# Two mixers of a one-core transformer kernel: low weight parts on another engine, branches interleaved, the triangular inverse spread between projections

## The chip, the cores and the metric

The kernel runs on one core of a Trainium2 chip. Such a core has TensorE (matmuls, written PE in the profile, its weight loads PEld), VectorE (DVE), ScalarE (ACT), GpSimd (POOL) and SyncE (SP), which here issues the transfers between memory and the core's own SBUF. Matmuls write to PSUM, which has eight banks. The metric is the time of one execution in microseconds (us).

## The reference

Two networks follow each other on 512 tokens of width 1024, all in float32. The first has two layers of: gated feed-forward, mixer, gated feed-forward; the second has attention, pooling, cross-attention and feed-forwards. Only the two mixers are touched. A mixer projects the normed tokens once and splits the columns:

```
proj = rmsnorm(x, mix_norm) @ w_in                     # 1024 -> 3600 columns
q, k, v, z, beta, alpha, hy = split(proj)
qkv  = silu(dwconv5(q, k, v));  q, k = l2norm(q), l2norm(k)
o_dn = delta_rule(q, k, v, beta, alpha), both directions  # chunked, needs the inverse of a
                                                       # unit triangular matrix per chunk and head
o_dn = rmsnorm(o_dn) * silu(z)
v, x1, x2 = dwconv3(hy) + bias                         # three streams
o_hy = rmsnorm(x2 * (h2 conv (x1 * (h1 conv v + d1 v)) + d2 ...))   # long filters by Fourier matrices
x = x + concat(o_dn, o_hy) @ w_out
```

## The kernel before, in words

**Precision by parts.** TensorE multiplies float32 matrices here in rounded form, so each operand is split in a high part (rounded by ScalarE) and a low part (the difference). A product is three matmuls (`acc3`, L330 to L336): high by high, high weight by low activation, low weight by high activation. For weights this is `load_w`: a transfer into `wr` (L302), then `split`: `wh` by ScalarE (L288) and `wl = wr - wh` (L289) by the engine that the caller names with `lo`. VectorE is the default; the mixer's projections name GpSimd.

**Projections of the mixer.** 28 weight tiles of 1024 x 128 (`proj`, 8 x 3 matmuls of 512 columns each): 12 heads (4 each of q, k, v), 12 streams of the hyena branch, 4 gates z. The result stands in a PSUM bank; VectorE multiplies it by the token norm `r`. A head then gets a convolution of five taps (`conv`: one on ScalarE, four on VectorE at L567), a tanh on ScalarE and a last product on VectorE; a stream three taps (two on VectorE); a gate a tanh and a product. Streams and gates are spilled to memory and read back later. A projection takes one of three PSUM banks (`pj`, `pj`, `pk`).

**Delta rule.** From k come per chunk of 128 tokens and per direction the matrices A (`decay`: matmuls, ScalarE's abs and exp, GpSimd's two mask products L864 and L868, VectorE's L866). `inverse` writes the 32 x 32 diagonal blocks of A to memory and reads them back with one block per partition (`L`), runs 31 steps of forward substitution on VectorE (two instructions each, L991 and L993), sends the result back through memory (L997 to L1004) and joins blocks by small matmuls (L1016 to L1042). `scan` then walks over four chunks in both directions (L1059 to L1095).

**Hyena.** `spectrum` makes the filters (L664, L665: high and low part of the filter's weights; L666 the decay, GpSimd's sums, L674 the transform). `hyena_run` convolves (L697, L715, L733) with products on VectorE (L719 to L742). The output projection is `half_proj`: first the half of its inputs from the delta rule, then the half from the hyena.

**What sets the order.** The program is recorded in the order of the code, and a scheduler then orders each engine's instructions by a model of their times, in the bounds of data, buffers and banks; each engine runs its own row in order. So code written later can stand earlier in a row. Transfers are all in SyncE's row.

Of the kernel before, what the change touches and what calls it, by code (L numbers as in the profile page):

```python
# [9 lines left out]
F32 = mybir.dt.float32  # L10
F32R = mybir.dt.float32r
ACTF = mybir.ActivationFunctionType
ALU = mybir.AluOpType
# [217 lines left out]
class Net:  # L231
# [395 lines left out]
    def filter_out(self, i, o, cs, th, tl):  # L627
        nc = self.nc
        wo = self.tmp("ssq", bufs=1)
        wov = self.a[f"flt{i}"][:, 196:].rearrange("p (d o c) -> p d o c", d=2, o=2)[:, :, o, cs]  # L630
        for e in range(2):
            nc.sync.dma_start(wo[64 * e:64 * e + 64].rearrange("p (d c) -> p d c", d=2), wov)
        wh = self.tmp(th, dt=F32R)
        wl = self.tmp(tl, dt=F32R)
        nc.scalar.copy(wh, wo)
        nc.vector.tensor_sub(wl[0:64], wo[0:64], wh[0:64].bitcast(F32))
        return wh, wl

    def spectrum(self, pool, i, hs, first, spec):
        nc, a = self.nc, self.a  # L640
# [12 lines left out]
        for o in range(2):  # L653
            for half in range(2):
                cs = slice(256 * half, 256 * half + 256)
                wh, wl = first if o == half == 0 else self.filter_out(i, o, cs, "t", "u")
                for lt in range(4):
                    dec, f = decs[n1 % 4], fb[n1 % 2]
# [3 lines left out]
                    for e, hs in ((0, fwd[lt]), (1, bwd[lt])):  # L662
                        es = slice(256 * e, 256 * e + 256)
                        nc.tensor.matmul(p[:, es], hs, wh[:, es], start=True, stop=False)  # L664
                        nc.tensor.matmul(p[:, es], hs[0:64], wl[0:64, es], start=False, stop=True)  # L665
                    nc.vector.tensor_mul(f, p.rearrange("p (d c) -> p d c", d=2), dec)  # L666
# [138 lines left out]
    def mixer(self, pool, i, spec, nrm):  # L805
        nc, a = self.nc, self.a
        win = a[f"win{i}"]
# [61 lines left out]

        for n, base, tag in (("k", 4, "k2"), ("v", 8, "v2"), ("q", 0, "q2")):  # L870
            qkv[n] = pool.tile([128, 4, S], F32, name=f"{n}2{i}", tag=tag)
            k2, v2 = qkv["k"], qkv.get("v")
            for h in range(4):
                p = self.proj(win[base + h], act, lo=nc.gpsimd)
                t, c, s = self.tmp("t"), self.tmp("u"), self.tmp("s")
                nc.vector.tensor_mul(t, p, r)
                self.conv(c, t, [self.col(f"dn_conv{i}", 12 * k + base + h) for k in range(5)])
                nc.scalar.activation(s, c, ACTF.Tanh, scale=0.5)
                nc.vector.scalar_tensor_tensor(qkv[n][:, h, :], s, 1.0, c, ALU.add, ALU.mult)
                if (n, h) == ("k", 1):  # L880
                    ba = self.mixer_small(i, act)
                elif (n, h) == ("v", 0):
                    pn["k"] = norms("k")
                elif (n, h) == ("v", 1):
                    be, g, G, ekd, egl, eg = self.mixer_gates(pool, i, ba, rt)
                elif n == "q":
                    if h == 0:
                        rates()
                    decay(h)
        Mc = self.inverse(pool, i, A, N)  # L890
        pn["q"] = norms("q")
        q2 = qkv["q"]
        nc.vector.tensor_scalar(epq, pn["q"], 4e-6, 1.28e-4, ALU.add, ALU.mult)
        for c in range(4):
# [4 lines left out]
            for d in range(2):  # L899
                nc.vector.tensor_tensor(at[:, d, c], hd(qk), at[:, d, c], ALU.mult)  # L900


# [15 lines left out]
        first = self.filter_out(i, 0, slice(0, 256), "a", "b")  # L918
        for t in range(3):
            for h in range(4):  # L920
                p = self.proj(win[16 + 4 * t + h], act, lo=nc.gpsimd)
                tt, c = self.tmp("t"), self.tmp("u")
                nc.vector.tensor_mul(tt, p, r)
                self.conv(c, tt, [self.col(f"hy_conv{i}", 12 * k + 4 * t + h) for k in range(3)],
                          self.col(f"hy_conv_bias{i}", 4 * t + h))
                nc.sync.dma_start(spill[(3, 0, 1)[t], h], c)
        for h in range(4):
            p = self.proj(win[12 + h], act, lo=nc.gpsimd)
            t, s = self.tmp("t"), self.tmp("s")
            nc.vector.tensor_mul(t, p, r)  # L930
            nc.scalar.activation(s, t, ACTF.Tanh, scale=0.5)
            nc.vector.scalar_tensor_tensor(t, s, 1.0, t, ALU.add, ALU.mult)
            nc.sync.dma_start(spill[2, h], t)

        o = pool.tile([128, 4, 4, 128], F32, name=f"o{i}", tag="v2")
# [32 lines left out]
    def inverse(self, pool, i, A, N):  # L968
# [17 lines left out]
        nc.gpsimd.memset(wf, 0.0)  # L986
        nc.gpsimd.memset(wf[:, 0:1024:33], 1.0)
        for k in range(31):
            n, m = 31 - k, k + 1
            t = T[:, 0:n * m].rearrange("p (a b) -> p a b", a=n)  # L990
            nc.vector.tensor_tensor(t, L[:, k + 1:, k:k + 1].to_broadcast([128, n, m]),  # L991
                                    W[:, k:k + 1, 0:m].to_broadcast([128, n, m]), ALU.mult)
            nc.vector.tensor_tensor(W[:, k + 1:, 0:m], W[:, k + 1:, 0:m], t, ALU.subtract)  # L993
        WT = pool.tile([128, 32, 32], F32, name=f"WT{i}", tag="L")
        nc.vector.tensor_copy(WT, W.rearrange("p r c -> p c r"))
# [592 lines left out]
```

## Time and profile before

| | us |
|---|---|
| median of three runs | 3795.7 (3792.1 to 3802.3) |
| the profiled execution's own time | 3800.8 |
| its span | 3799.0 |
| TensorE, VectorE, ScalarE, GpSimd busy | 3684.7, 2122.5, 1341.5, 976.1 |
| first mixer: first and last matmul of its projections | 392.6 to 640.6 |
| second mixer: the same | 1583.8 to 1827.9 |

A window of the profile gives for each engine its busy time and instructions, and the granted clock of TensorE as a share of 2.4 GHz. A matmul's row shows a duration longer than the distance to the next, since matmuls overlap; rates are therefore taken from counts in a stretch or from starts that follow each other. "a <- b" in a wait is the instruction that waited and what ended its wait.

### The profile page before, as it was taken

What the parts mean: (1) busy time and instruction counts of PE and PEld (TensorE: products, weight loads), DVE (VectorE), ACT (ScalarE), POOL (GpSimd) and SP (SyncE); (2) the same over time, 40 slices, a digit from 0 to 9 for tenths busy, and PEclk for the clock granted to TensorE, in tenths of its full rate; (3) what the DMA queues carried; (4) which work ended last, traced back from release to release, by engine and by line L of the source; (5) the groups of instructions that cost most, each with busy time, mean ns of one, the idle gap of its engine ahead of it and who ended that gap; (6) DMA issues with size and microseconds to landing.
All of it is one profiled execution on the core that took longest, in us unless ns stands there. A gap on an engine that the chain in (4) does not pass through costs nothing.

```text
span 3799.0 us, 45466 instructions
## 1 busy us (share of the span) xinstructions
PE 3684.7 (97%) x17516; PEld 2969.6 (78%) x17516; DVE 2122.5 (56%) x3190; ACT 1341.5 (35%) x2009; POOL 976.1 (26%) x705
## 2 busy tenths in 40 slices
PE   8999989999999999998999999999999999899998
PEld 6878767888888878767887888877788888688886
DVE  4344695774334443486675344667666464866464
ACT  3223432133223323352223233346444343444342
POOL 2111353431021201253442112477101011510011
PEclk9999998999999999998999999999999999999999
DMA  3232333522323233423343232410423334323322
GB/s 119 89 101 88 126 106 108 168 78 94 94 92 94 91 95 91 143 81 114 116 161 98 88 110 90 135 40 32 142 90 106 95 94 121 118 68 95 94 94 83
DMA packets 178816, 383.95 MB, mean 101 GB/s; under 512 B 40550, under 2 KB 83302, under 8 KB 177576
## 3 DMA queue, kind: packets, MB, share of 16 engines
q1 hardware_dynamic: 178600, 381.06, 32.1%
q8 instruction: 137, 2.24, 0.3%
q14 instruction: 79, 0.65, 0.1%
HBM read 347.97 MB, written 33.03 MB: 100 GB/s over the span
## 4 chain that ended last, share of the span: by engine, by line
PE 83%; DVE 11%; issue 2%; DMA 2%; ACT 2%; POOL 1%; SPq 0%; DVEq 0%; ACTq 0%; POOLq 0%
PE pj L331 10%; PE pj L330 10%; PE pj L336 8%; PE pk L331 5%; PE pk L330 5%; PE pa L330 4%; PE ps L330 4%; PE pa L331 4%; PE ps L331 4%; PE ps L336 4%; PE pa L336 4%; PE pk L336 4%; DVE u L567 3%; PE pj L333 2%; PE pk L333 1%
## 5 line engine op out<-in xcount | busy, mean ns | idle before, releaser
L288 ACT CAST wh<-wr 128x1024 fp32r<-128x1024 f32 x612 | 590.2, 964 | 1146.3 <-PE pj L331 462.6
L289 DVE TENSOR_TENSOR wl<-wr,wh 128x1024 fp32r<-128x1024 f32 (+1 forms) x554 | 626.6, 1131 | 483.0 <-PE pj L336 125.7
L514 POOL TENSOR_TENSOR t<-s,u 128x512 f32<-128x512 f32 x88 | 175.9, 1999 | 1072.9 <-DVE u L513 967.6
L331 PE MATMUL pj<-xl_ffn_norm,wh 128*128 128x512 f32 x856 | 339.8, 397 | 3.9 <-DVE xl_ffn_norm L292 3.9
L330 PE MATMUL pj<-xh_ffn_norm,wh 128*128 128x512 f32 x856 | 339.3, 396 | 0.0
L375 POOL TENSOR_TENSOR ssq<-ssq,c 128x512 f32<-128x512 f32 x76 | 113.3, 1491 | 489.2 <-ACT c L372 460.0
L336 PE MATMUL pj<-xh_ffn_norm,wl 128*128 128x512 f32 x856 | 217.7, 396 | 0.0
L289 POOL TENSOR_TENSOR wl<-wr,wh 128x1024 fp32r<-128x1024 f32 x58 | 146.9, 2534 | 225.6 <-ACT wh L288 195.0
L548 POOL TENSOR_TENSOR t<-t,s 128x512 f32<-128x512 f32 x44 | 58.0, 1318 | 569.2 <-DVE s L567 499.9
L331 PEld LDWEIGHTS pj<-xl_ffn_norm,wh 128*128 128x128 f32 x856 | 161.1, 188 | 44.3 <-DVE xl_ffn_norm L292 6.0
L330 PEld LDWEIGHTS pj<-xh_ffn_norm,wh 128*128 128x128 f32 x856 | 161.3, 188 | 40.6 <-issue 1.6
L336 PEld LDWEIGHTS pj<-xh_ffn_norm,wl 128*128 128x128 f32 x856 | 160.9, 188 | 39.1 <-issue 0.8
L288 ACT CAST hh_ffn_norm<-t 128x512 fp32r<-128x512 f32 x132 | 81.5, 618 | 307.2 <-POOL t L514 303.0
L330 PE MATMUL pk<-xh_ffn_norm,wh 128*128 128x512 f32 x472 | 187.1, 396 | 0.6 <-ACT wh L288 0.6
L567 DVE SCALAR_TENSOR_TENSOR u<-t,vec,u 128x511 f32<-128x511 f32 (+1 forms) x144 | 169.9, 1188 | 31.1 <-ACT u L561 22.0
L331 PE MATMUL pk<-xl_ffn_norm,wh 128*128 128x512 f32 x472 | 187.0, 396 | 0.0
L289 DVE TENSOR_TENSOR hl_ffn_norm<-t,hh_ffn_norm 128x512 fp32r<-128x512 f32 x132 | 92.2, 699 | 164.7 <-ACT hh_ffn_norm L288 164.7
L331 PE MATMUL pj<-hl_ffn_norm,wh 128*128 128x512 f32 x396 | 157.0, 397 | 0.0
L330 PE MATMUL pj<-hh_ffn_norm,wh 128*128 128x512 f32 x396 | 156.9, 396 | 0.0
L330 PE MATMUL ps<-xh_ffn_norm,wh 128*128 128x512 f32 x384 | 152.6, 397 | 0.0
L330 PE MATMUL pa<-xh_ffn_norm,wh 128*128 128x512 f32 x384 | 152.4, 397 | 0.0
L331 PE MATMUL ps<-xl_ffn_norm,wh 128*128 128x512 f32 x384 | 152.2, 396 | 0.0
(792 smaller groups left out, 8689.7 us busy)
## 6 DMA issues: line engine op xcount, KB each, us to landing
wr<-in_cu SPq DMA_DIRECT2D x88, 512.0 KB, 3.5
wr<-in_win SPq DMA_DIRECT2D x56, 512.0 KB, 3.6
wr<-in_ffn2g SPq DMA_DIRECT2D x44, 512.0 KB, 3.5
wr<-in_ffn2u SPq DMA_DIRECT2D x44, 512.0 KB, 3.5
wr<-in_ffn1g SPq DMA_DIRECT2D x43, 512.0 KB, 3.4
wr<-in_ffn1u SPq DMA_DIRECT2D x43, 512.0 KB, 3.5
wr<-in_ffn1d SPq DMA_DIRECT2D x32, 512.0 KB, 3.5
wr<-in_ffn2d SPq DMA_DIRECT2D x32, 512.0 KB, 3.5
```

The lines of the kernel that those rows point to most:

```text
L288: nc.scalar.copy(h, src)
L289: lo.tensor_sub(l, src, h.bitcast(F32))
L330: mm(out, sh, mh, start=first and i == 0, stop=False)
L331: mm(out, sh, ml, start=False, stop=False)
L333: mm(out, sl, mh, start=False, stop=last and i == n - 1)
L336: mm(out, sl, mh, start=False, stop=last and i == n - 1)
L375: (nc.gpsimd if k < n - 1 else nc.vector).tensor_add(ssq, ssq, sq)
L514: nc.gpsimd.tensor_mul(t, s, u)
L548: nc.gpsimd.tensor_mul(t, t, cs[1])
L567: nc.vector.scalar_tensor_tensor(out[:, a:b], t[:, a + d:b + d], taps[k], out[:, a:b], ALU.mult, ALU.add)
```

## The change

The 28 projections of a mixer no longer name GpSimd, so `wl` falls to VectorE. Heads and streams alternate in the code: four k heads with the first four streams, four v heads with the next four, together with `decay`. `inverse` becomes a generator that yields after each step, and the four gates, the last four streams and the four q heads are written between its steps, three steps after each. The gate's result goes to another buffer. The low part of the filter's weights is made on all 128 partitions instead of 64 and multiplied with all of `hs`.

```diff
@@ -633,7 +633,7 @@
         wh = self.tmp(th, dt=F32R)
         wl = self.tmp(tl, dt=F32R)
         nc.scalar.copy(wh, wo)
-        nc.vector.tensor_sub(wl[0:64], wo[0:64], wh[0:64].bitcast(F32))
+        nc.vector.tensor_sub(wl, wo, wh.bitcast(F32))
         return wh, wl
 
     def spectrum(self, pool, i, hs, first, spec):
@@ -662,7 +662,7 @@
                     for e, hs in ((0, fwd[lt]), (1, bwd[lt])):
                         es = slice(256 * e, 256 * e + 256)
                         nc.tensor.matmul(p[:, es], hs, wh[:, es], start=True, stop=False)
-                        nc.tensor.matmul(p[:, es], hs[0:64], wl[0:64, es], start=False, stop=True)
+                        nc.tensor.matmul(p[:, es], hs, wl[:, es], start=False, stop=True)
                     nc.vector.tensor_mul(f, p.rearrange("p (d c) -> p d c", d=2), dec)
                     nc.gpsimd.tensor_add(eo[lt][:, 0], f[:, 0], f[:, 1])
                     nc.gpsimd.tensor_sub(eo[lt][:, 1], f[:, 0], f[:, 1])
@@ -867,29 +867,62 @@
                                                    ALU.mult, ALU.mult)
                 nc.gpsimd.tensor_mul(at[:, d, c], E, self.mats[:, 1 + d, None, :].to_broadcast([128, 4, 128]))
 
-        for n, base, tag in (("k", 4, "k2"), ("v", 8, "v2"), ("q", 0, "q2")):
+        for n, tag in (("k", "k2"), ("v", "v2"), ("q", "q2")):
             qkv[n] = pool.tile([128, 4, S], F32, name=f"{n}2{i}", tag=tag)
-            k2, v2 = qkv["k"], qkv.get("v")
-            for h in range(4):
-                p = self.proj(win[base + h], act, lo=nc.gpsimd)
-                t, c, s = self.tmp("t"), self.tmp("u"), self.tmp("s")
-                nc.vector.tensor_mul(t, p, r)
-                self.conv(c, t, [self.col(f"dn_conv{i}", 12 * k + base + h) for k in range(5)])
-                nc.scalar.activation(s, c, ACTF.Tanh, scale=0.5)
-                nc.vector.scalar_tensor_tensor(qkv[n][:, h, :], s, 1.0, c, ALU.add, ALU.mult)
-                if (n, h) == ("k", 1):
-                    ba = self.mixer_small(i, act)
-                elif (n, h) == ("v", 0):
-                    pn["k"] = norms("k")
-                elif (n, h) == ("v", 1):
-                    be, g, G, ekd, egl, eg = self.mixer_gates(pool, i, ba, rt)
-                elif n == "q":
-                    if h == 0:
-                        rates()
-                    decay(h)
-        Mc = self.inverse(pool, i, A, N)
+        k2, v2, q2 = qkv["k"], qkv["v"], qkv["q"]
+
+        def head(n, h):
+            base = {"k": 4, "v": 8, "q": 0}[n]
+            p = self.proj(win[base + h], act)
+            t, c, s = self.tmp("t"), self.tmp("u"), self.tmp("s")
+            nc.vector.tensor_mul(t, p, r)
+            self.conv(c, t, [self.col(f"dn_conv{i}", 12 * k + base + h) for k in range(5)])
+            nc.scalar.activation(s, c, ACTF.Tanh, scale=0.5)
+            nc.vector.scalar_tensor_tensor(qkv[n][:, h, :], s, 1.0, c, ALU.add, ALU.mult)
+
+        def stream(m):
+            t, h = m // 4, m % 4
+            p = self.proj(win[16 + m], act)
+            tt, c = self.tmp("t"), self.tmp("u")
+            nc.vector.tensor_mul(tt, p, r)
+            self.conv(c, tt, [self.col(f"hy_conv{i}", 12 * k + m) for k in range(3)],
+                      self.col(f"hy_conv_bias{i}", m))
+            nc.sync.dma_start(spill[(3, 0, 1)[t], h], c)
+
+        def gate(h):
+            p = self.proj(win[12 + h], act)
+            t, s, z = self.tmp("t"), self.tmp("s"), self.tmp("u")
+            nc.vector.tensor_mul(t, p, r)
+            nc.scalar.activation(s, t, ACTF.Tanh, scale=0.5)
+            nc.vector.scalar_tensor_tensor(z, s, 1.0, t, ALU.add, ALU.mult)
+            nc.sync.dma_start(spill[2, h], z)
+
+        for h in range(4):
+            head("k", h)
+            stream(h)
+            if h == 1:
+                ba = self.mixer_small(i, act)
+            elif h == 2:
+                be, g, G, ekd, egl, eg = self.mixer_gates(pool, i, ba, rt)
+        pn["k"] = norms("k")
+        head("v", 0)
+        rates()
+        for c in range(4):
+            stream(4 + c)
+            decay(c)
+            if c < 3:
+                head("v", 1 + c)
+        inv = self.inverse(pool, i, A, N)
+        fill = [lambda h=h, f=f: f(h) for h in range(4)
+                for f in (gate, lambda h: stream(8 + h), lambda h: head("q", h))]
+        next(inv)
+        for n, step in enumerate(fill):
+            step()
+            for _ in range(3):
+                next(inv, None)
+        for _ in inv:
+            pass
         pn["q"] = norms("q")
-        q2 = qkv["q"]
         nc.vector.tensor_scalar(epq, pn["q"], 4e-6, 1.28e-4, ALU.add, ALU.mult)
         for c in range(4):
             cs = slice(128 * c, 128 * c + 128)
@@ -898,7 +931,6 @@
                 nc.tensor.matmul(hd(qk)[:, h], k2[:, h, cs], q2[:, h, cs], start=True, stop=True)
             for d in range(2):
                 nc.vector.tensor_tensor(at[:, d, c], hd(qk), at[:, d, c], ALU.mult)
-
 
         KV = pool.tile([128, 2, 4, 4, 128], F32, name=f"KV{i}", tag="A")
         for t, src in ((0, k2), (1, v2)):
@@ -916,22 +948,6 @@
 
         hs = self.hidden(pool, i)
         first = self.filter_out(i, 0, slice(0, 256), "a", "b")
-        for t in range(3):
-            for h in range(4):
-                p = self.proj(win[16 + 4 * t + h], act, lo=nc.gpsimd)
-                tt, c = self.tmp("t"), self.tmp("u")
-                nc.vector.tensor_mul(tt, p, r)
-                self.conv(c, tt, [self.col(f"hy_conv{i}", 12 * k + 4 * t + h) for k in range(3)],
-                          self.col(f"hy_conv_bias{i}", 4 * t + h))
-                nc.sync.dma_start(spill[(3, 0, 1)[t], h], c)
-        for h in range(4):
-            p = self.proj(win[12 + h], act, lo=nc.gpsimd)
-            t, s = self.tmp("t"), self.tmp("s")
-            nc.vector.tensor_mul(t, p, r)
-            nc.scalar.activation(s, t, ACTF.Tanh, scale=0.5)
-            nc.vector.scalar_tensor_tensor(t, s, 1.0, t, ALU.add, ALU.mult)
-            nc.sync.dma_start(spill[2, h], t)
-
         o = pool.tile([128, 4, 4, 128], F32, name=f"o{i}", tag="v2")
         self.scan(pool, i, o, k2, q2, KV, at, N, c1, ekd, egl, eg)
         self.spectrum(pool, i, hs, first, spec)
@@ -985,12 +1001,14 @@
         wf = W.rearrange("p r c -> p (r c)")
         nc.gpsimd.memset(wf, 0.0)
         nc.gpsimd.memset(wf[:, 0:1024:33], 1.0)
+        yield
         for k in range(31):
             n, m = 31 - k, k + 1
             t = T[:, 0:n * m].rearrange("p (a b) -> p a b", a=n)
             nc.vector.tensor_tensor(t, L[:, k + 1:, k:k + 1].to_broadcast([128, n, m]),
                                     W[:, k:k + 1, 0:m].to_broadcast([128, n, m]), ALU.mult)
             nc.vector.tensor_tensor(W[:, k + 1:, 0:m], W[:, k + 1:, 0:m], t, ALU.subtract)
+            yield
         WT = pool.tile([128, 32, 32], F32, name=f"WT{i}", tag="L")
         nc.vector.tensor_copy(WT, W.rearrange("p r c -> p c r"))
         nc.sync.dma_start(sv[1, 0:64], WT[0:64])
```

How rows move, in the first mixer. VectorE, in the middle of the inverse before (L991 and L993 are its steps, u a tap of a convolution, pj a projection's bank):

```order
L567 SCALAR_TENSOR_TENSOR u409_4154<-t408_4153,vec_69,u409_4154 128x511
L993 TENSOR_TENSOR W0_3438<-W0_3438,T0_3439 128x16x16
L567 SCALAR_TENSOR_TENSOR u409_4154<-t408_4153,vec_69,u409_4154 128x511
L991 TENSOR_TENSOR T0_3439<-L0_3437,W0_3438 128x255
L993 TENSOR_TENSOR W0_3438<-W0_3438,T0_3439 128x15x17
L991 TENSOR_TENSOR T0_3439<-L0_3437,W0_3438 128x252
L993 TENSOR_TENSOR W0_3438<-W0_3438,T0_3439 128x14x18
L923 TENSOR_TENSOR t412_4191<-pj410_4160,r238_2630 128x512
```

and in the changed kernel, where the steps are L1008 and L1010:

```order
L289 TENSOR_TENSOR wl388_3909<-wr388_3907,wh388_3908 128x1024
L1008 TENSOR_TENSOR T0_3575<-L0_3573,W0_3574 128x231
L567 SCALAR_TENSOR_TENSOR u380_3846<-t379_3845,vec_69,u380_3846 128x510
L1010 TENSOR_TENSOR W0_3574<-W0_3574,T0_3575 128x21x11
L567 SCALAR_TENSOR_TENSOR u380_3846<-t379_3845,vec_69,u380_3846 128x511
L1008 TENSOR_TENSOR T0_3575<-L0_3573,W0_3574 128x240
L567 SCALAR_TENSOR_TENSOR u380_3846<-t379_3845,vec_69,u380_3846 128x511
L1010 TENSOR_TENSOR W0_3574<-W0_3574,T0_3575 128x20x12
L567 SCALAR_TENSOR_TENSOR u380_3846<-t379_3845,vec_69,u380_3846 128x510
L895 TENSOR_TENSOR t384_3893<-pk382_3862,r238_2630 128x512
L1008 TENSOR_TENSOR T0_3575<-L0_3573,W0_3574 128x247
L289 TENSOR_TENSOR wl392_3953<-wr392_3951,wh392_3952 128x1024
```

Between the steps stood the taps of a stream; now stand there the four taps of a head, the start of a gate (L895), and a low weight part for each projection.

TensorE at the first matmuls of the inverse (N, A) before:

```order
L1016 MATMUL pa344_3575<-N0_2647,A0_2645 32x32 x16
L1016 MATMUL ps345_3593<-N0_2647,A0_2645 32x32 x16
L1023 MATMUL ps346_3611<-P10_3538,Mc0_3440 32x32 x16
L1023 MATMUL pa347_3629<-P10_3538,Mc0_3440 32x32 x16
L330 MATMUL pj434_4388<-xh_mix_norm00_2552,wh435_4390 128x512
```

and changed:

```order
L674 MATMUL pj532_4940<-eo03_4798,ftab00_4807 128x256
L674 MATMUL pj533_4950<-eo03_4798,ftab01_4809 128x256
L1034 MATMUL pa405_4105<-N0_2647,A0_2645 32x32 x16
L1034 MATMUL pa407_4141<-N0_2647,A0_2645 32x32 x16
L674 MATMUL pk534_4960<-eo00_4795,ftab01_4809 128x256
```

The matmuls of the inverse were followed by the projections of the four gates (pj434 is the first); now they stand between transforms of the spectrum (eo, ftab), behind all projections.

TensorE at the start of the output projection (xh_o, xl_o) before:

```order
L733 MATMUL pj625_5628<-inv011_5150,yt0121_5541 128x256 x2
L733 MATMUL pk629_5646<-inv000_5144,yt0130_5594 128x256 x2
L330 MATMUL pj676_5832<-xh_o00_5666,wh675_5827 128x512
L331 MATMUL pj676_5832<-xl_o00_5667,wh675_5827 128x512
L333 MATMUL pj676_5832<-xh_o00_5666,wl675_5828 128x512
L330 MATMUL pj676_5832<-xh_o01_5668,wh675_5827 128x512
```

and changed:

```order
L733 MATMUL pk633_5650<-inv011_5154,yt0131_5599 128x256 x2
L974 MATMUL ps654_5742<-mats_70,o0_4540 128x128
L974 MATMUL ps657_5753<-mats_70,o0_4540 128x128 x3
L974 MATMUL pa660_5764<-mats_70,o0_4540 128x128 x4
L974 MATMUL ps663_5775<-mats_70,o0_4540 128x128 x4
L330 MATMUL pj680_5836<-xh_o00_5670,wh679_5831 128x512
```

The projection began inside the last hyena block (L733); now it follows that block and the transposes of the scan's output (L974).

## Rows read from the trace of the kernel before

**Rows 1.** The page, part 1: TensorE's busy time, share of the span, instructions.

```profile
PE 3684.7 (97%) x17516; PEld 2969.6 (78%) x17516; DVE 2122.5 (56%) x3190; ACT 1341.5 (35%) x2009; POOL 976.1 (26%) x705
```

**Rows 2.** Windows: stretch, length, engines' busy us (instructions), PE's granted clock, DMA share, GB/s.

```profile
412.00:580.00 168.00, 145.59 (x644) 110.37 (x641) 152.63 (x238) 71.40 (x121) 82.90 (x40) 0.97 0.32 96
580.00:640.00 60.00, 59.11 (x597) 48.68 (x598) 23.29 (x28) 16.93 (x26) 15.81 (x11) 0.82 0.33 91
640.00:721.00 81.00, 80.98 (x472) 68.29 (x471) 55.27 (x96) 17.31 (x37) 33.62 (x39) 0.98 0.47 142
721.00:785.00 64.00, 62.30 (x443) 58.44 (x442) 53.56 (x134) 13.52 (x28) 33.10 (x39) 1.00 0.47 150
...
1620.00:1790.00 170.00, 150.42 (x888) 118.75 (x887) 139.16 (x222) 66.53 (x113) 79.12 (x39) 0.93 0.36 104
1790.00:1850.00 60.00, 60.00 (x409) 47.66 (x407) 30.63 (x43) 19.70 (x33) 21.61 (x19) 0.97 0.30 95
```

**Rows 3.** TensorE's waits, 392 to 640 us: total us, times, longest.

```profile
PE pj L333 <- POOL wl L289: 5.8, 5, 1.7
```

**Rows 4.** SyncE's waits, 400 to 600 us.

```profile
SPq L302 <- POOL wl L289: 80.6, 12, 10.3
```

**Rows 5.** VectorE groups, 412 to 580 us: shapes, count, busy us, mean ns, idle before.

```profile
L567 DVE SCALAR_TENSOR_TENSOR u<-t,vec,u 128x511 f32<-128x511 f32 x46 | 54.4, 1186 | 3.6 <-ACT u L561 2.8
L567 DVE SCALAR_TENSOR_TENSOR u<-t,vec,u 128x510 f32<-128x510 f32 x24 | 28.8, 1211 | 2.5 <-ACT u L559 2.3
...
L923 DVE TENSOR_TENSOR t<-pj,r 128x512 f32<-128x512 f32 x8 | 5.5, 683 | 0.0
```

**Rows 6.** Timeline: start us, duration us, instruction.

```profile
538.61 0.74 DVE L567 SCALAR_TENSOR_TENSOR u<-t,vec,u 128x511 f32<-128x511 f32 x1
...
539.41 2.51 POOL L289 TENSOR_TENSOR wl<-wr,wh 128x1024 fp32r<-128x1024 f32 x1 [4.44 <-ACT wh L288]
539.60 2.88 DVE L567 SCALAR_TENSOR_TENSOR u<-t,vec,u 128x511 f32<-128x511 f32 x1
```

**Rows 7.** GpSimd's groups, 392 to 640 us.

```profile
L289 POOL TENSOR_TENSOR wl<-wr,wh 128x1024 fp32r<-128x1024 f32 x28 | 70.1, 2504 | 114.7 <-ACT wh L288 105.2 <-DMA wr<-in_win 4.8 <-PE pj L333 2.4
L868 POOL TENSOR_TENSOR at<-b,mats 128x512 f32<-128x512 f32 x8 | 13.4, 1681 | 0.0
```

**Rows 8.** VectorE's groups, 620 to 800 us: its own low weight parts.

```profile
L289 DVE TENSOR_TENSOR wl<-wr,wh 128x1024 fp32r<-128x1024 f32 x4 | 4.9, 1221 | 0.4 <-ACT wh L288 0.4
```

**Rows 9.** Chain of waits, 568 to 584 us: start us, us, what.

```profile
571.73 3.26 DMA scr<-W
...
582.80 1.21 PE ps L1016 x19
```

**Rows 10.** Window in a stretch without idle time of TensorE, columns as in rows 2.

```profile
360.00:392.00 32.00, 32.00 (x138) 25.78 (x138) 12.38 (x16) 11.24 (x16) 6.34 (x5) 1.00 0.38 117
```

**Rows 11.** VectorE's groups of the spectrum, 580 to 721 us.

```profile
L666 DVE TENSOR_TENSOR fb<-pj,spk 128x512 f32<-128x512 f32 x10 | 6.8, 684 | 3.2 <-PE pj L665 1.9 <-POOL eo L668 1.3
...
L683 DVE TENSOR_TENSOR so<-so,pj 128x256 f32<-128x256 f32 x10 | 4.0, 412 | 0.0
...
L636 DVE TENSOR_TENSOR u<-ssq,t 64x512 fp32r<-64x512 f32 x3 | 2.8, 938 | 0.6 <-ACT t L635 0.6
```

**Rows 12.** Timeline of TensorE: two filter products of the spectrum.

```profile
641.34 0.38 PE L664 MATMUL pk<-a,hs 128*128 128x256 f32 x1
641.65 0.38 PE L665 MATMUL pk<-b,hs 64*128 64x256 f32 x1
```

**Rows 13.** Chain of waits, 380 to 830 us: transforms of the spectrum.

```profile
649.02 1.73 PE pj L674 x8
```

**Rows 14.** Single lines: durations min/median/max, then first and last start us.

```profile
L1067 PE MATMUL ps<-KV,N x8: 274/276/276, 648.0 to 648.7; 128*128 128x128 f32 x8
...
L1067 PE MATMUL pa<-a,N x8: 275/276/276, 721.1 to 721.9; 128*128 128x128 f32 x8
...
L330 PE MATMUL pj<-xh_o,wh x15: 392/396/585, 784.1 to 799.4; 128*128 128x512 f32 x15
```

## Prediction

> **What bounds the kernel now.** I read the page first: TensorE is busy 97% of the span [rows 1], so time can only come from stretches where it idles or runs slow. A table of stretches finds them in the two mixers [rows 2]. In the first mixer, from 412 us (where the token norm r is ready and VectorE can begin) to 580 us, TensorE is busy 145.6 of 168 us at a granted clock of 0.97: 22.4 us idle and 0.03 x 168 = 5.0 us of clock. From 580 to 640 us it is 0.9 us idle, but the clock is 0.82, another 10.8 us: it stands at 1.2 instead of 2.4 GHz for part of that time, after TensorE had waited for the inverse. That is 39 us. The same sum over 1620 to 1850 us in the second mixer gives 19.6 + 11.9 + 0 + 1.8 = 33 us. These 72 us are all that smoother mixers could win there. VectorE is the other side: it is busy 152.6 of the 168 us, while from 580 us on it needs well under half, and later 55 of 81 us.
>
> Then I asked who makes TensorE and the weights wait. The longest wait of TensorE for another compute engine in this stretch is for wl, the low weight part that GpSimd makes at L289 [rows 3], and the queue that loads the weights (SyncE) stands 80.6 us behind the same instruction, since the raw tile is free only after it [rows 4]. Last, the groups of VectorE by shape: one convolution tap (L567) takes 1186 and 1211 ns in the mean over 70 instructions, although one takes 0.74 us when undisturbed [rows 5, 6]. The timeline shows why: at 539.41 GpSimd starts a 2.51 us wl, and the tap that starts at 539.60 lasts 2.88 us, until GpSimd is done [rows 6]. The multiply by r, which reads one of its operands from PSUM, keeps its 683 ns throughout [rows 5].
>
> The Trainium skill (SBUF — State Buffer, section "Who interferes with whom") says that a VectorE instruction with two SBUF inputs and a GpSimd instruction that reads SBUF exclude each other, the later one waiting for the whole of the earlier. The tap has two SBUF inputs and the multiply one; the trace agrees with 2.88 against 0.74 us for the first and 683 ns for the second.
>
> **Part 1: low weight parts go to VectorE.** Removed per mixer: 28 GpSimd instructions of 2.5 us [rows 7]. What they cost VectorE: the taps alone lose 46 x (1186 - 740) + 24 x (1211 - 740) ns = 32 us, and steps of the inverse and other two-operand rows are hit too; at 2.88 - 0.74 = 2.1 us a hit, 28 hits would be 59 us. Between 32 and 59 I take 40 us, since some of the 28 fall where VectorE has nothing to do. Added per mixer: 28 instructions on VectorE at 1.22 us, the one of this shape that it already makes near a mixer [rows 8]. Five of them stand ahead of 412 us, where VectorE waits anyway; two more, of the output weights, now stand inside the stretch: 25 x 1.22 = 30.5 us. Net for VectorE: -9.5 us. The waits of TensorE and of the load queue for GpSimd go away; what they wait for next is VectorE's own place in line.
>
> **Part 2: branches interleaved, inverse spread.** Before, twelve heads (four taps each) come first, then the hyena streams and gates (two taps or none), of which four gates run after the vector steps of the inverse, among its matmuls. Now heads alternate with streams, and the 31 steps of the inverse lie between gates, the last streams and the query heads. In TensorE's new row all 28 projections, and then the first part of the spectrum, stand ahead of the first matmul of the inverse.
>
> When does the inverse end? Before, its last vector step ends at 571.7 us and the round trip through DRAM brings the first matmul on the whole to 582.8 us, 11 us later [rows 9]. Now VectorE has in front of that step: -40 + 30.5 from part 1; three streams that used to come behind it, 3 x (0.68 + 2 x 0.75) = 6.5 us; four gates of two instructions of 0.68 us, 5.5 us; and of the spectrum six products of 0.68, eight sums of 0.41 and two weight parts of 0.94 us, 9 us [rows 5, 11]. Sum: 571.7 + 11.5 = 583, and the first matmul at 594 us. So the inverse is 11.5 us **later**.
>
> What has TensorE done more by then? One projection is 24 matmuls at 32/138 = 0.232 us each [rows 10], 5.6 us; four gates are 22 us. Of the spectrum come first half of the filter products, 32 matmuls at 0.31 us [rows 12], and 28 of the 128 transforms at 1.73/8 = 0.216 us [rows 13], 16 us. Together 38 us, which just fits: 27.4 us were lost in this stretch, and it is 11.5 us longer. Lead: 38 - 11.5 = 26.5 us.
>
> What is given back? (a) The matmuls of the inverse keep their 11.7 us of slow clock and idle time; I change nothing, as the wait for the round trip stays. (b) Before, the scan lay beside the spectrum (first matmul 648.0, last about 722 us, [rows 14]), where VectorE was at 55 of 81 us, and the hyena convolutions came after. Now the scan lies beside the hyena, where VectorE is already at 53.6 of 64 us. The scan adds some 25 instructions of 0.69 us (17 us) on VectorE and 272 matmuls of about 0.11 us (half the pitch of a 256-column one, 30 us) on TensorE: 71 of 94 us, not a bound, but two chains that cross on one engine in order. From nothing to 10 us, I take 5. (c) At the end the scan's output was normalised long before the last hyena block, so that the first output projection, at 784.1 us [rows 14], covered that block. Now the last products and splits of the scan's output (four and four, about 0.7 us each as others of their size in [rows 5]) stand behind the last hyena sums on VectorE: about 5 us in which TensorE has nothing, between 0 and 8. So 26.5 - 10 = 16.5 us per mixer.
>
> The 64 added rows of the filter's low part change no length: instruction and matmul run over the same columns. The activation tables are loaded as often as before.
>
> **Sum.** Two mixers: 2 x 16.5 = 33 us. The profiled execution took 3800.8 us (span 3799.0, 1.8 around it), so 3768 us on its scale; the median of the runs is 5 us lower, which gives **3762 us**. Bounds on the terms: 32 or 59 instead of 40 moves the inverse 8 us later or 19 earlier; (b) and (c) between 0 and 18. The likeliest case's own range is 3740 to 3785.
>
> **Rivals.**
> *TensorE bound throughout.* If VectorE keeps up everywhere, also in the matmuls of the inverse (the spectrum fills its waits and the clock stays at 2.4 GHz), all 72 us come back: 3724 us. For it: VectorE's and TensorE's work between 412 and 583 us are nearly equal now. Against: the round trip stands still in a fixed row of TensorE. Chance 0.15.
>
> *VectorE takes it back.* The wl are two-operand instructions themselves and now meet the 16 mask products that GpSimd keeps (1.68 us, [rows 7]) and the products of the inverse. If 20 us of the 40 come back that way, the inverse ends 31 us later than before, the lead is 38 - 31 = 7 us and (b), (c) eat it: 3790 to 3798 us, no change. For it: VectorE is at 91% before. Against: the mask products are outside the inverse, and only 8 hits of theirs would make 16 us. Chance 0.14.
> The Trainium skill (Perfetto Trace Analysis, section "Optimizing Scalar/DVE Operations") says that a saturated VectorE may be relieved by handing work to GpSimd, with a warning that it might not help, as the two share a port. Read as advice, it speaks against this change and for this rival; by it the sum would be 30.5 us worse per mixer. The warning is what the 2.88 us row shows.
>
> *The scan beside the hyena is the new chain (slower).* Scan start to output projection was 784 - 648 = 136 us with spectrum, scan and hyena in it. After the first matmul of the inverse there is left before the scan: the rest of the spectrum, 32 x 0.31 + 100 x 0.216 = 31 us, and what stood between 582.8 and 648 us without the four gates and the 16 filter products, 65 - 22 - 5 = 38 us. So the scan starts at 594 + 69 = 663 us, and the projection can't start before it ends. (With 64 us of hyena, 30 of scan and 10 of (b) and (c) the forecast's projection starts at 767 us, 17 before 784.) A step took 74/4 = 18.5 us; if it doubles under the hyena's VectorE load, the scan ends at 663 + 148, and with 10 us for the norm the projection starts at 821 instead of 784 us: 37 us lost per mixer, 3870 us at worst. It decides from (784 - 663 - 10)/4 = 28 us a step. Against: two directions in turn, and a step has only three products on VectorE in a row. Chance 0.08.
>
> **How the numbers follow.** Forecast 0.63, the others 0.15, 0.14 and 0.08. The range takes in the first two rivals' times: 3722 to 3796. A measurement here tells 0.3% (11 us) from no change. Faster by more: forecast and TensorE-bound case, with a little of the third, 0.80; within: 0.12; slower: 0.08.
>
> **What would show it.** In the profile after: no wl on GpSimd, taps of 0.75 us in the mean, wl of 1.2 us on VectorE; no wait of TensorE for GpSimd's wl; the last inverse step near 583 us and its first matmul near 594 us, with spectrum matmuls before it; TensorE over 95% busy from 412 to 580 us; a hole of some 5 us before the output projection. It is wrong if taps stay above 1 us (then something else on GpSimd blocked them), if the inverse's step ends after 595 us, or if the scan's steps exceed 28 us.

## The result, and the profile after

The changed kernel takes 3741.4 us (median of 4 runs, 3735.8 to 3748.3), the kernel before 3798.9 us (4 runs of the same session): a ratio of 0.9856, 95% interval 0.9841 to 0.9871, or 57 us less. The forecast was 3762 us, so the direction is right, and the gain larger than the 33 us that the sum gave. The profiled execution took 3748.3 us, 52.5 less than the one before. The two mixers share this unequally: from its first projection to its first output projection the first is 29.5 us shorter (361.9 instead of 391.4 us), the second 14.7 (375.1 instead of 389.8).

The page, part 1, of the changed kernel, and the table of stretches that answers to [rows 1, 2] (same columns):

```profile
PE 3654.4 (98%) x17516; PEld 2955.9 (79%) x17516; DVE 2084.2 (56%) x3246; ACT 1342.5 (36%) x2009; POOL 826.4 (22%) x649
```

```profile
412.00:580.00 168.00, 165.58 (x758) 129.66 (x756) 140.59 (x263) 80.13 (x130) 28.60 (x23) 0.99 0.38 120
580.00:640.00 60.00, 54.47 (x563) 45.83 (x561) 29.31 (x60) 12.75 (x27) 20.88 (x26) 0.82 0.56 146
640.00:721.00 81.00, 79.77 (x610) 74.22 (x610) 59.52 (x118) 16.62 (x33) 34.10 (x40) 1.00 0.35 108
721.00:785.00 64.00, 61.72 (x357) 53.09 (x356) 51.82 (x112) 19.70 (x35) 21.26 (x21) 1.00 0.32 108
...
1620.00:1790.00 170.00, 161.45 (x1011) 133.58 (x1010) 125.18 (x239) 63.39 (x111) 45.64 (x44) 0.92 0.46 134
1790.00:1850.00 60.00, 55.85 (x412) 48.78 (x410) 32.31 (x66) 14.81 (x29) 20.51 (x24) 0.94 0.43 123
```

From 412 to 580 us TensorE idles 2.4 instead of 22.4 us. From 580 to 640 us it idles 5.5 instead of 0.9 us, at the same low clock: the stretch around the inverse has become worse. The last two rows do not cover the same work as in [rows 2], since the second mixer now starts at 1550.0 instead of 1583.8 us. In the first row VectorE is now busy 140.6 us, 12 less, though 26 low weight parts were added to it.

VectorE's groups of the changed kernel from 412 to 580 us (answer to [rows 5]); then TensorE's waits from 392 to 640 us and SyncE's from 400 to 600 us (answers to [rows 3, 4]: total us, times, longest):

```profile
L567 DVE SCALAR_TENSOR_TENSOR u<-t,vec,u 128x511 f32<-128x511 f32 x46 | 34.6, 757 | 1.0 <-ACT u L561 0.5
L289 DVE TENSOR_TENSOR wl<-wr,wh 128x1024 fp32r<-128x1024 f32 x26 | 32.5, 1251 | 1.0 <-ACT wh L288 1.0
L567 DVE SCALAR_TENSOR_TENSOR u<-t,vec,u 128x510 f32<-128x510 f32 x23 | 17.1, 742 | 1.8 <-ACT u L559 1.8
```

```profile
PE pa L1034 <- DMA N<-scr: 2.6, 1, 2.6
PE pj L674 <- DVE so L683: 1.3, 1, 1.3
PE pk L674 <- POOL eo L667: 1.2, 1, 1.2
```

```profile
SPq L302 <- DVE wl L289: 69.7, 14, 8.2
```

The taps are back at 0.75 us in the mean. TensorE waits for no `wl` any more; what it waits for now lies behind the projections. The load queue still stands 69.7 us behind `wl` (80.6 before), now VectorE's, and it costs nothing: TensorE does not wait for weights. A long wait in a queue is no loss by itself.

Where the steps of the first mixer lie (single lines: durations min/median/max, first and last start us): the copy behind the inverse's last step, its first matmuls, the first and last of the scan's, the first output projection, in the changed kernel.

```profile
L1013 DVE COPY WT<-W x1: 1456/1456/1456, 591.8 to 591.8; 128x1024 f32<-128x1024 f32 x1
...
L1034 PE MATMUL pa<-N,A x64: 236/236/257, 601.6 to 604.8; 32*32 32x32 f32 x64
...
L1085 PE MATMUL ps<-KV,N x8: 273/275/275, 659.3 to 660.1; 128*128 128x128 f32 x8
...
L1085 PE MATMUL pa<-a,N x8: 275/275/275, 731.1 to 731.8; 128*128 128x128 f32 x8
...
L330 PE MATMUL pj<-xh_o,wh x44: 395/396/501, 753.8 to 801.8; 128*128 128x512 f32 x44
```

The inverse is later than forecast (601.6, not 594), and the output projection earlier (753.8, not 767). From the inverse's matmuls to the projection it takes 152 us where the forecast had 173.

The filter products of the spectrum, TensorE's timeline in the changed kernel (answer to [rows 12]):

```profile
567.46 0.28 PE L664 MATMUL pk<-a,hs 128*128 128x256 f32 x1
567.58 0.28 PE L665 MATMUL pk<-b,hs 128*128 128x256 f32 x1
567.70 0.28 PE L664 MATMUL pk<-a,hs 128*128 128x256 f32 x1
```

Their starts lie 0.12 us apart; before, 0.31 us. Nothing in the prediction foresaw this.

### The profile page after: what moved, and what is told of

Same layout as the page of the kernel before. It is cut to its first block, busy times and chain, and to the rows that moved or that the text cites. A ratio compares the mean times of both kernels' runs of the same rounds, so it can differ in the third digit from the quotient of the medians.

```text
span 3746.4 us, 45394 instructions
## 1 busy us (share of the span) xinstructions
PE 3654.4 (98%) x17516; PEld 2955.9 (79%) x17516; DVE 2084.2 (56%) x3246; ACT 1342.5 (36%) x2009; POOL 826.4 (22%) x649
## 4 chain that ended last, share of the span: by engine, by line
PE 91%; DVE 4%; issue 2%; DMA 1%; ACT 1%; POOL 1%; SPq 0%; DVEq 0%; ACTq 0%; POOLq 0%
PE pj L330 12%; PE pj L331 12%; PE pj L336 8%; PE pk L330 6%; PE pk L331 6%; PE ps L330 4%; PE pa L330 4%; PE ps L331 4%; PE pa L331 4%; PE ps L336 4%; PE pa L336 4%; PE pk L336 4%; PE pj L333 4%; PE pk L333 2%; PE pj L715 1%
## 5 line engine op out<-in xcount | busy, mean ns | idle before, releaser
L289 DVE TENSOR_TENSOR wl<-wr,wh 128x1024 fp32r<-128x1024 f32 x610 | 695.1, 1140 | 509.4 <-PE pj L336 125.7
L336 PEld LDWEIGHTS pj<-xh_ffn_norm,wl 128*128 128x128 f32 x856 | 160.6, 188 | 39.6 <-issue 0.8
L331 PE MATMUL pa<-xl_ffn_norm,wh 128*128 128x512 f32 x384 | 151.9, 396 | 0.0
L333 PE MATMUL pj<-xh_mix_norm,wl 128*128 128x512 f32 x304 | 120.8, 397 | 0.0
```

The costliest lines, as they stand in the source:

```text
L289: lo.tensor_sub(l, src, h.bitcast(F32))
L331: mm(out, sh, ml, start=False, stop=False)
L333: mm(out, sl, mh, start=False, stop=last and i == n - 1)
L336: mm(out, sl, mh, start=False, stop=last and i == n - 1)
```

## Experiments

All were timed against the kernel before. The theory after reading the two traces: the gain is made of the stalls behind GpSimd and of the filter's rows, and the new order adds little or costs. The rival: the order fills TensorE, as the prediction's sum had it.

| kernel | median us | ratio to before, 95% |
|---|---|---|
| e1: 128 filter rows only | 3773.9 | 0.9936 (0.9924 to 0.9948) |
| e2: low parts on VectorE only | 3748.8 | 0.9877 (0.9861 to 0.9892) |
| e3: both, old order | 3724.7 | 0.9807 (0.9794 to 0.9821) |
| the change: both, new order | 3741.4 | 0.9856 (0.9841 to 0.9871) |
| e4: the change, 64 filter rows | 3763.7 | 0.9908 (0.9894 to 0.9923) |
| e5: the change, inverse earlier | 3726.6 | 0.9801 (0.9783 to 0.9818) |
| e6: the change, inverse first | 3726.0 | 0.9812 (0.9798 to 0.9826) |
| e7: the change, low parts on GpSimd | 3768.0 | 0.9927 (0.9913 to 0.9941) |
| e8: e2 with idle work on GpSimd | 3827.2 | 1.0074 (1.0061 to 1.0087) |
| e9: the change, 64 and 64 rows | 3755.1 | 0.9887 (0.9872 to 0.9902) |
| e10: e4, high, low, low, high | 3755.9 | 0.9885 (0.9868 to 0.9901) |

**e1, one edit to the kernel before.**

```diff
-        nc.vector.tensor_sub(wl[0:64], wo[0:64], wh[0:64].bitcast(F32))
+        nc.vector.tensor_sub(wl, wo, wh.bitcast(F32))
-        nc.tensor.matmul(p[:, es], hs[0:64], wl[0:64, es], start=False, stop=True)
+        nc.tensor.matmul(p[:, es], hs, wl[:, es], start=False, stop=True)
```

> The kernel before, with one edit: the low part of the filter products runs over 128 rows instead of 64, the third edit of the change, which the prediction priced at nothing. Theory (from the two traces: 128 of these matmuls have 384 ns and follow each other at 0.31 us where 64-row and 128-row tiles alternate, 276 ns and about 0.1 us where all have 128 rows): TensorE loses time at each change of the tile's rows; 128 x 0.2 = 26 us at most, and since TensorE is nearly full there, 14 to 26 us faster than before: 3773 to 3785 us. Rival (the prediction's price): the matmuls cost the same and were only disturbed by their neighbours in the kernel before; within 5 us of before, and what the change gained beyond the forecast comes from the order.

Measured: 0.64% or 24 us less. From start to start, the 128 filter products of both mixers take 19.2 instead of 39.6 us, which is 20 of the 24. The theory holds; the prediction's price of nothing does not.

**e2, the low weight parts alone.** The argument `lo=nc.gpsimd` is dropped in the three calls of `proj` in `mixer`.

> The kernel before, with the low weight parts of the mixers' 28 projections on VectorE, the old order and the old 64 filter rows. Theory (the prediction's part 1): about 40 us of stalls a mixer go and 30.5 us of work come, so taps fall from 1.19 to about 0.75 us and the inverse's last vector step comes some 10 us earlier; 15 to 25 us faster than before in both mixers: 3774 to 3784 us. Rival A (VectorE takes it back): same within 5 us. Rival B (the wait for GpSimd was itself the larger cost, TensorE and the load queue included): over 30 us faster.

Measured: 1.23% or 47 us less, beyond what the theory gave and within rival B. The single line of the copy behind the inverse's last step in e2 (in the kernel before it starts at 571.7 us), the taps from 412 to 580 us, and the windows of the front:

```profile
L995 DVE COPY WT<-W x1: 1118/1118/1118, 561.8 to 561.8; 128x1024 f32<-128x1024 f32 x1
```

```profile
L567 DVE SCALAR_TENSOR_TENSOR u<-t,vec,u 128x511 f32<-128x511 f32 x48 | 40.9, 859 | 0.4
...
L567 DVE SCALAR_TENSOR_TENSOR u<-t,vec,u 128x510 f32<-128x510 f32 x24 | 21.2, 893 | 0.6 <-ACT u L559 0.5
```

```profile
412.00:560.00 148.00, 143.75 (x649) 111.98 (x648) 137.74 (x257) 72.64 (x122) 26.11 (x18) 0.98 0.34 106
560.00:640.00 80.00, 80.00 (x704) 63.14 (x703) 36.88 (x57) 23.00 (x39) 20.60 (x22) 0.87 0.44 119
```

The copy starts 9.9 us earlier than before, near the 9.5 us of part 1, but not by the same sum: ahead of it stand 22 low parts instead of 25, and all 12 streams instead of 9. The taps do not fall to 0.75 us as expected, but to 0.86 and 0.89: in this order eleven of the 72 taps still run beside GpSimd's mask products (L864, L868), which costs them 9 us in all. In the changed kernel none does. From 412 to 640 us TensorE idles 4.3 us, against 23.3 us in the kernel before ([rows 2], 22.4 + 0.9). These 19 us are most of the 24.7 us by which the first mixer is shorter (from its first projection to its first output projection, 366.7 instead of 391.4 us). So TensorE's idle time goes without any new order in the source. Rival B is right in size; its cause is tested by e8. The row of TensorE moved all the same: only one projection is left among the inverse's matmuls, instead of four, since the instruction order is set by simulated times and not by the source alone.

**e3, both local edits in the old order.** The edits of e1 and e2 together.

> The kernel before with the low weight parts on VectorE and 128 filter rows, in the old order: the changed kernel without its new order. Theory: the two local edits make most of the gain, 30 to 45 us faster than before (3754 to 3769 us), and the order gives the remaining 12 to 25 us, since only it fills TensorE between the start of VectorE's work and the inverse. Rival (order is the whole gain beyond the stalls): no more than 20 us faster than before, 3779 us or above.

Measured: 3724.7 us, 1.93% less than before, and below the changed kernel with intervals that don't meet. The gains of e1 and e2 add up (24 + 47 = 71 of 73 us). The theory's first half is right; its second, that the order gives another 12 to 25 us, is wrong in sign: the new order costs about 17 us.

**e4, the filter's low part back on 64 rows.** The edits of e1, undone in the changed kernel.

> The changed kernel with the low part of the filter products back on 64 rows. Theory: each change of rows costs TensorE again, 128 x 0.2 = 26 us at most, some of it in idle time around the inverse: 12 to 26 us slower than the changed kernel, 3753 to 3767 us, which is what the prediction's sum gave without this term. Rival: no difference, 3741 us.

Measured: 3763.7 us, 22 us slower than the change by the medians, 20 by the ratios, and 2 us from the forecast of 3762.

**e5, the inverse earlier.** Four v heads go behind the inverse's start.

```diff
-        head("v", 0)
         rates()
         for c in range(4):
             stream(4 + c)
             decay(c)
-            if c < 3:
-                head("v", 1 + c)
...
-                for f in (gate, lambda h: stream(8 + h), lambda h: head("q", h))]
+                for f in (lambda h: head("v", h), gate, lambda h: stream(8 + h), lambda h: head("q", h))]
```

> The changed kernel with the four v heads moved behind the start of the inverse (into the stretch with gates, last streams and q heads): on VectorE 15 projections instead of 19 stand ahead of the inverse's first step, as in the kernel before. All else as changed. Theory (from the two traces and the run in the old order): the changed kernel is 17 us slower than its own local edits in the old order because four more projections at TensorE's pace of 5.6 us, 22 us, stand ahead of the inverse, so that its round trip and small matmuls find no projection left beside them. Then the last vector step comes near 568 instead of 590.7 us, TensorE loses some 8 instead of 21 us behind 560 us, and the time is 10 to 25 us below the changed kernel: 3716 to 3731 us. Rival (the tail costs it: scan beside hyena, hole before the output projection): as the changed kernel, 3736 to 3746 us.

Measured: 3726.6 us, as e3. The copy (its line of e5 stands below) comes at 572.3 instead of 591.8 us, the inverse's first matmul at 580.7 instead of 601.6, the output projection at 742.5 instead of 753.8. The scan (L1082, 637.9 to 713.3 us) still lies beside the hyena (L733, from 673.7), as in the changed kernel, so the rival (the tail costs it) falls.

```profile
L1010 DVE COPY WT<-W x1: 1129/1129/1129, 572.3 to 572.3; 128x1024 f32<-128x1024 f32 x1
```

What the spread of the inverse does by itself needs no run: with all steps at once, or five after each projection instead of three, the rows of all five engines come out word for word as in the changed kernel, apart from numbers. That edit of the diff does nothing; the scheduler spreads the steps anyway, as it did before.

**e6, the first four streams moved behind too.** 11 projections ahead of the inverse.

> As the last kernel, and the first four streams moved too: 11 projections ahead of the inverse (four k heads without streams between them, a stream before each decay). Theory: another four projections earlier, so the inverse's matmuls have six or more projections beside them; the remaining idle time behind the last vector step goes, another 5 to 10 us per mixer at most: 3700 to 3725 us. Rival (VectorE bounds the front): four heads of four taps in a row and the decays take VectorE longer than TensorE, PSUM banks stay full, and TensorE loses in front what it wins behind: 3725 to 3750 us.

Measured: 3726.0 us, no more than e5 gave, and just past the theory's range. The copy comes at 558.1 us, but from 460 to 500 us TensorE idles 3.4 us (none in the change). Between 11 and 15 projections ahead of it, the place of the inverse no longer shows in the time.

**e7, the low weight parts of the change back on GpSimd.** `lo=nc.gpsimd` in `head`, `stream` and `gate`.

> The changed kernel with the low weight parts of the 28 projections on GpSimd again: new order and 128 filter rows alone. Theory (stalls behind GpSimd): some 40 us of stalls a mixer come back on VectorE and 30.5 us of work go; as VectorE has 27 us of idle time between 412 and 560 us in the changed kernel, part of it is covered: 15 to 47 us slower than the changed kernel, 3756 to 3788 us, taps at 1.1 us or more in the mean. Rival (the new order alone fills TensorE, whatever VectorE does): no slower, 3741 us.

Measured: 3768.0 us, 27 us slower than the change, with taps at 1.39 (42 of them) and 0.98 us (20) from 412 to 580 us. Against e1 (same low parts and rows, old order, 0.9936) the order's 0.9927 is no difference that these intervals show. So with the stalls the order neither helps nor hurts measurably, and without them it costs.

**e8, idle work on GpSimd.** e2, and after each `split` of the 28:

```diff
+            self.nc.gpsimd.tensor_sub(self.idle, h.bitcast(F32), self.idle)
```

> The kernel before with the low weight parts on VectorE (as in the run of that edit alone, 3749 us), and beside each of the 28 a subtraction of the same size on GpSimd whose result nobody uses: it reads the high weight part and a scratch tile and writes the scratch tile. So TensorE and the load queue never wait for GpSimd, but VectorE's two-input instructions meet GpSimd as before. Theory (the stalls are the cost): about 40 us of stalls a mixer come back while the 30.5 us of work stay, so it is slower than the run without the dummy by 40 to 80 us in all: 3789 to 3829 us, taps at 1.1 us or more. Rival (the cost was that TensorE and the load queue waited for a weight part made by GpSimd): 3745 to 3755 us, taps at 0.75 us.

Measured: 3827.2 us, 78 us slower than e2. No other instruction uses these results. What waits for the subtractions themselves is ScalarE, twice in the whole run (4.2 us, for the `wh` that they read), and GpSimd's own mask products, twice (2.2 us). The timeline of VectorE and GpSimd in this kernel:

```profile
536.54 0.74 DVE L569 SCALAR_TENSOR_TENSOR u<-t,vec,u 128x511 f32<-128x511 f32 x1
537.03 2.76 POOL L305 TENSOR_TENSOR idle<-wh,idle 128x1024 f32<-128x1024 f32 x1 [4.72 <-ACT wh L288]
537.43 2.90 DVE L569 SCALAR_TENSOR_TENSOR u<-t,vec,u 128x511 f32<-128x511 f32 x1
```

A tap that starts 0.40 us into the subtraction lasts 2.90 us, as in [rows 6], the taps' mean from 412 to 580 us is 1148 and 1112 ns, and VectorE is busy 163.5 of these 168 us. So it is the meeting of the two engines that costs, and not that TensorE or the load queue waits for GpSimd. This is what the Trainium skill (SBUF — State Buffer, section "Who interferes with whom") says of two-input instructions and GpSimd; the trace agrees, with 2.90 against 0.74 us.

**e9 and e10, rows of the filter products.** e9 takes `hs[0:64]` and the first 64 rows of `wh` and `wl` in both products. e10 is e4 with the second half of a bank in turned order:

```diff
+                        two = ((hs, wh[:, es]), (hs[0:64], wl[0:64, es]))
+                        for n, (x, w) in enumerate(two if e == 0 else two[::-1]):
+                            nc.tensor.matmul(p[:, es], x, w, start=n == 0, stop=n == 1)
```

> The changed kernel with both products of the filter over 64 rows: the low half of hs and of the weights' rows is left out of both, so the result lacks a low-order term and its time alone is of interest. Theory (the change of rows from one matmul to the next is what costs): no change of rows any more, so as fast as 128 and 128: 276 ns each, 3736 to 3747 us. Rival (a matmul over 64 rows is slow in itself): 384 ns, as the run with 128 and 64 rows by turns, 3758 to 3770 us, or slower, since now all 128 + 128 have it.

> The changed kernel with the low products on 64 rows (as the run at 3764 us), but in the order high, low, low, high within a bank, so that the number of rows changes twice instead of four times a bank. Theory: half of the 22 us comes back: 3748 to 3758 us, and of the matmuls about half stay at 276 to 300 ns. Rival (64 rows cost by themselves, not the change): 3760 to 3768 us.

The three forms in TensorE's timeline, first 128 and 64 rows by turns (e4), then 64 and 64 (e9):

```profile
568.13 0.28 PE L664 MATMUL pk<-a,hs 128*128 128x256 f32 x1
568.34 0.38 PE L665 MATMUL pk<-b,hs 64*128 64x256 f32 x1
568.65 0.38 PE L664 MATMUL pk<-a,hs 128*128 128x256 f32 x1
568.96 0.38 PE L665 MATMUL pk<-b,hs 64*128 64x256 f32 x1
```

```profile
567.95 0.27 PE L665 MATMUL pk<-b,hs 64*128 64x256 f32 x1
568.06 0.28 PE L664 MATMUL pk<-a,hs 64*128 64x256 f32 x1
568.18 0.28 PE L665 MATMUL pk<-b,hs 64*128 64x256 f32 x1
```

With 64 rows throughout they follow at 0.11 to 0.12 us, exactly as with 128; from a matmul between two changes of rows to the next start it is 0.31, and from one with a change on one side 0.21 (568.13 to 568.34). So 64 rows aren't slow, the change is: about 0.2 us each. The change of the stationary matrix is not the cause: in the changed kernel the second pair of a bank has another `hs` than the first, and it follows at the same 0.12 us (567.58 to 567.70). e10, with half the changes, lies at 3755.9 us, where half of e4's loss would put it, though its interval overlaps both e4's and the change's, so that the time alone does not decide; its 128 filter products take 33.9 us from start to start, between e4's 46.3 and the change's 23.2. The time of e9, 3755.1, lies above its 3736 to 3747: the matmuls cost what they should (23.6 us in all), but with other rows the scheduler laid another order around the inverse, where TensorE's clock is 0.79 from 560 to 640 us (0.85 in the change). What of the 14 us is clock and what is place was not taken apart.

## Why the prediction was right, and where it failed

**Part 1** is right in its mechanism (e8). Its sum is near the truth, in part by luck. The taps did lose 32 us, but not to the low parts alone: of the 24 taps over 0.95 us in the kernel before, 16 run beside a low part (some 26 us lost) and 8 beside a mask product (some 8). The net gain of 9.5 us shows as 9.9 us at the end of the inverse in e2, with other terms (see there). The rival that VectorE takes it back is out as a time. Its meeting with the mask products is real, 9 us a mixer in the old order (e2); the new order keeps the two apart, with taps at 757 and 742 ns. What the prediction missed is what this is worth. It priced part 1 only through the end of the inverse; but without the stalls TensorE also idles 19 us less in the first mixer, for 9.9 us at the inverse (e2). Alone it is worth 47 us, where 2 x 9.5 = 19 of the forecast's 33 us were its share.

**Part 2** was credited with the other 14 us and costs about 15 (e4 against e2; 17, e3 against the change). Right: TensorE is busy 98.6% from 412 to 580 us, no projection is left for later. Wrong: the time of the inverse, 591.8 instead of 583. The round trip was taken a little too long, which hardly matters: the prediction put the inverse's first matmul on the whole at 582.8 us, 11 us after the last step, but in the kernel before the first of them starts at 580.3, 8.6 us after the copy (9.8 in the changed kernel).

```profile
L1016 PE MATMUL pa<-N,A x64: 235/236/258, 580.3 to 586.0; 32*32 32x32 f32 x64
```

The sum counted VectorE's instructions, as if VectorE were still the one that is full; in the window from 412 to 560 us of the changed kernel it idles 26.6 us, TensorE 0:

```profile
412.00:560.00 148.00, 148.00 (x683) 116.18 (x680) 121.41 (x231) 73.86 (x122) 22.78 (x18) 1.00 0.37 116
```

The inverse's steps stand in VectorE's row behind 19 projections instead of 15, and so come at TensorE's pace: four more of 5.6 us are 22 us, and e5, which takes these four away, gets 19.5 of them back. The lead of 26.5 us was credited to the order; the old order loses no more once the stalls are gone (TensorE idles 4.3 us from 412 to 640 us in e3, 7.9 in the change). In the change 29 us lie between the last projection (572.8) and the inverse's first matmul, with nothing but the spectrum for TensorE, and waits in it; in e5 they are 9 us, and in e3 projections go on to 598 us, beside the inverse.

**What is given back.** (a) The inverse keeps its slow clock, and gets 4.6 us more idle time in that stretch. (b) The scan beside the hyena costs close to nothing: TensorE is busy 141.5 of 145 us from 640 to 785 us. The slower rival is out: the scan takes 72.5 us (659.3 to 731.8), 18.1 us a step, where the rival needed 28. (c) The hole before the output projection is small: TensorE idles 0.65 us from 740 to 760 us in the first mixer. In the second it idles 3.4 us from 1905 to 1930 us, and there the granted clock is 0.86, another 3.5 us, which is part of why that mixer gained less.

**The step that failed** is the sentence "The 64 added rows of the filter's low part change no length: instruction and matmul run over the same columns." It is worth 20 to 24 us (e1, e4), the whole difference between the forecast and the result: with 64 rows the change takes 3763.7 us. The sign stood in the rows: [rows 12] have 0.31 us from one 256-column matmul to the next, while [rows 10] give 0.232 us for 512 columns. The prediction took the 0.31 over as a price and did not ask why half the columns take longer. That the rest of the sum met is partly chance: part 1 was too small by 28 us (19 against 47), and part 2 too good by 29 (14 gained against 15 lost).

The TensorE-bound rival's 3724 us is reached by e3 and e5, but only with the 24 us of the filter rows, which it did not count: not all of its 72 us came back in any run.

## What to carry to other kernels

Price an edit of a matmul's shape from the start-to-start times of its rows, and when a matmul over fewer columns takes longer than one over more, look at its neighbours. When a change relieves the bounding engine, ask which engine sets the pace next, and time every moved step by that one's. Split a change into its parts on the chip: the best kernel here (e3, 3724.7 us, with e5 and e6 beside it) is the change without its new order.

## What the hardware showed that was not expected

A change between 64-row and 128-row matmuls costs TensorE about 0.2 us here, half on each side of it (with 256 columns 0.12, 0.21 and 0.31 us from start to start with none, one and two changes beside a matmul).

TensorE's granted clock falls in the inverse even when TensorE never idles. The inverse's first matmuls of e3, and its windows, same columns as above:

```profile
L1016 PE MATMUL pa<-N,A x64: 191/191/212, 572.0 to 574.9; 32*32 32x32 f32 x64
```

```profile
560.00:570.00 10.00, 10.00 (x44) 8.04 (x44) 5.81 (x7) 3.16 (x4) 0.00 (x0) 1.00 0.87 221
570.00:580.00 10.00, 10.00 (x213) 9.31 (x212) 1.03 (x3) 2.31 (x4) 0.00 (x0) 0.76 0.77 173
580.00:590.00 10.00, 10.00 (x112) 8.88 (x110) 5.12 (x7) 2.35 (x4) 0.00 (x0) 0.50 0.28 92
590.00:600.00 10.00, 10.00 (x80) 8.24 (x81) 2.14 (x4) 2.72 (x5) 2.13 (x3) 0.89 0.10 38
```

Projections run until 572.0 us, then the inverse's 32-row matmuls begin. Already from 570 to 580 us the mean clock is 0.76, and from 580 to 590 us it is at 1.2 GHz (0.50), though TensorE is busy throughout. The prediction had put the low clock down to the wait for the round trip; that wait is not needed for it: in e3 TensorE has no idle time from 560 to 640 us.
